# The gated MLP's up projection: the rest of each weight block from an accumulating fetch onto its negated head

## The chip, the cores and the metric

The kernel runs on one core of a Trainium2 chip. The metric is the device time of one launch in microseconds (us), as the median of several runs; the runs shown here were 954.19, 954.41 and 954.55 us. Beside them stands one profiled execution, whose span from the first to the last instruction is 952.6 us. Engines are called as in the profile: PE is TensorE (PEld its weight loads), DVE is VectorE, ACT is ScalarE, POOL is GpSimd, and SP is SyncE, which issues most of the transfers.

## What is computed

One layer of a hybrid decoder on 512 tokens of 1024 channels: three token mixers, a gated merge, an output projection, and a gated MLP with a short causal convolution. The change touches the MLP's first product, `h2 @ w_up`, whose weights are 1024 x 6144 numbers of 4 bytes.

```python
    h2 = rms_norm(x, norm_ffn[l])
    up = causal_dwconv(h2 @ w_up[l], ffn_conv_w[l], ffn_conv_b[l])
    gate_h, val_h = jnp.split(up, 2, axis=-1)
    x = x + (jax.nn.gelu(gate_h, approximate=True) * val_h) @ w_down[l]
return rms_norm(x, final_norm)
```

## The kernel before

**Products in three parts.** Every large product runs in a 4-byte format (`float32r`) that keeps 12 bits of each number. To hold more, each operand is kept as two tiles: its 12-bit head and the exact rest, which again fits the format. `split` (L92) makes them: ACT writes the head (L94, a copy with rounding), and DVE subtracts the head from the source (L95). `mm3` (L97) then multiplies head by head, head by rest, and rest by head, in that order: for a tile of 128 output channels and 8 tiles of input channels it first issues the 16 products of the weights' head and then the 8 of the weights' rest (L101, 24 matmuls in all).

**Units and steps.** The kernel is a list of units, each a block of weights and what PE does with it, with steps of other work between them. `unit` (L130) and `step` (L134) put them on the list, `weave` (L137) mixes them, and `emit` (L169) walks it. Ahead of a unit, `emit` calls `fetch` for the blocks up to two units later (`AHEAD`). `fetch` (L149) issues the load of a block into a buffer `raw` on SP's queue (L152; there are three such buffers) and the `split`. Blocks with `parts` 1 have their head and rest in `whi` and `wlo`, of which there are three each. Blocks with `parts` 2 have them in four half-size tiles `r` out of a common pool of 53 slots of 128 x 512 numbers (L77), from which most activations come too. Buffers are handed out in the order of the program; the order of the instructions on each engine is fixed by a planner before the run, by that same order as far as a buffer and the operands are expected to be free.

**The MLP** runs in three groups (L958). Each group has 16 up units (`up_units`, L928), two for each of 8 tiles of hidden channels (one for the gate half, one for the value half), and then 8 down units (`down_units`, L855), which add the group's part of the second product to the residual `x2`. An up unit is 24 matmuls with `h2` as the activations, and `up_done` (L918): the convolution of three taps over the product (one ACT instruction, L910, two DVE instructions, L912), and for each second unit the gelu (L922, ACT), the product of both halves (L923, DVE) and a `split` of the result.

**The entry to the MLP.** The first three up units of the first group are `early` ones (L933, `parts` 2): they run the first 256 tokens while the norm of the last tokens is still being made. `norm2` and `norm2_flip` (L883, L887) make the normed activations: a mean square (ACT), some small steps (DVE), two scalings (DVE, L877), a transposition on PE (L895) and a `split` into `h2h` and `h2l`. The other 13 units of the first group and all 32 of the other two have `parts` 1: 45 units in all.

**The end.** Behind the last down units `final` (L949) makes the last norm and stores the result; it holds the one arithmetic instruction that POOL has in the MLP (L951).

Of the kernel before, what the change touches and what calls it, by code (L numbers as in the profile page):

```python
# [20 lines left out]
KD = D // P  # L21
# [17 lines left out]
AHEAD = 2  # L39
BRANCHES = (2, 0, 1)  # L40
# [3 lines left out]
# columns of the packed per-channel parameters  # L44
# [10 lines left out]
def trunk(ctx: ExitStack, tc: tile.TileContext, x, xT, mem, memT, par, wdecay, wch, wvd, wvg, wmk,  # L55
# [35 lines left out]
    # ---------------------------------------------------------------- helpers  # L91
    def split(hi, lo, src, eng=None):  # L92
        """src as its 12-bit head and the exact rest."""
        nc.scalar.activation(hi, src, AF.Copy)  # L94
        (eng or nc.vector).tensor_tensor(out=lo, in0=src, in1=hi.bitcast(F32), op=ALU.subtract)  # L95

    def mm3(ps, terms, first=True, last=True):  # L97
        """ps (+)= sum of lhsT.T @ rhs over (lhsT_hi, lhsT_lo, rhs_hi, rhs_lo)."""
        seq = [p for a, b, c, d in terms for p in ((a, c), (a, d))] + [(b, c) for a, b, c, d in terms]
        for i, (l, r) in enumerate(seq):  # L100
            nc.tensor.matmul(ps, lhsT=l, rhs=r, start=first and i == 0,  # L101
                             stop=last and i == len(seq) - 1)

    def rsqrt(v):
        """1 / sqrt(v) of [p, n] positive numbers: a guess from the exponent, three Newton steps."""
        n = v.shape[-1]
        y, h, t = stat(n), stat(n), stat(n)
        yi = y.bitcast(I32)
        nc.vector.tensor_scalar(out=yi, in0=v.bitcast(I32), scalar1=1, scalar2=None, op0=ALU.logical_shift_right)
        nc.vector.tensor_scalar(out=yi, in0=yi, scalar1=-1, scalar2=0x5F3759DF, op0=ALU.mult, op1=ALU.add)  # L110
        nc.vector.tensor_scalar(out=h, in0=v, scalar1=-0.5, scalar2=None, op0=ALU.mult)
        for _ in range(3):
            nc.vector.tensor_tensor(out=t, in0=y, in1=y, op=ALU.mult)
            nc.vector.tensor_tensor(out=t, in0=t, in1=h, op=ALU.mult)
            nc.vector.scalar_tensor_tensor(out=y, in0=t, scalar=1.5, in1=y, op0=ALU.add, op1=ALU.mult)
        return y

    def meansq(src, acc, width):
        """acc = sum of src^2 / width along the rows."""
        junk = small.tile([P, src.shape[-1]], BF16, tag="junk", name=nm("junk"), bufs=2)  # L120
        nc.scalar.activation(junk, src, AF.Square, scale=width ** -0.5, accum_out=acc)

    # ---------------------------------------------------------------- the program: a list of units, each a block
    # of weights and what the tensor engine does with it, and of steps of other work between them. A unit's
    # weights are fetched and split two units ahead of it.
    prog = []
    loads = []
    behind = {}  # loads issued behind the weights of a unit

    def unit(dram, n, fn, parts=1):  # L130
        """fn(W): W(j, m) is the [128, n/m] hi and lo part j of m of the [128, n] block."""
        prog.append((dram, n, fn, parts))

    def step(fn):  # L134
        prog.append((None, 0, fn, 0))

    def weave(units, steps, lead=0):  # L137
        """The units with the steps spread evenly behind them, from unit `lead` on."""
        done, m = 0, max(1, len(units) - lead)
        for i, u in enumerate(units):  # L140
            unit(*u)
            upto = len(steps) * max(0, i + 1 - lead) // m
            for s in steps[done:upto]:
                step(s)
            done = max(done, upto)
        for s in steps[done:]:
            step(s)

    def fetch(dram, n, parts):  # L149
# [10 lines left out]
        for j in range(2):  # L160
            ts.append((rslot((p, h)), rslot((p, h))))
            split(*ts[j], raw[:, j * h:(j + 1) * h])
# [6 lines left out]
    def emit():  # L169
        units = [i for i, p in enumerate(prog) if p[0] is not None]  # L170
        ws, at = {}, 0
        for i, (dram, n, fn, parts) in enumerate(prog):
            if dram is None:
                fn()
                continue
            u = units.index(i)
            while at < len(units) and at <= u + AHEAD:
                p = prog[units[at]]
                ws[units[at]] = fetch(p[0], p[1], p[3])
                for h in behind.get(at, ()):  # L180
                    h()
                at += 1
            fn(ws.pop(i))

    # ---------------------------------------------------------------- constants
# [7 lines left out]
    # keeps the tensor engine busy, and its clock up, until the first loads are in  # L193
# [10 lines left out]
    def add_square(acc, a):  # L204
        """acc + a^2 / 1024, for the rows' mean squares"""
# [6 lines left out]
    def mean_square(acc, n):  # L212
        """[128, n] mean squares, plus eps, of n*128 rows from the sums over 1024/128 tiles of their transpose."""
# [6 lines left out]
    def row_bcast(rstd, n):  # L220
        """[128, n*128] tile whose column t*128+i holds rstd[i, t] in every partition."""
# [14 lines left out]
    def token_units(dram, n, lhs, nt, evac):  # L236
        """Units for evac(t, psum[128 tokens, n]) of activations @ a block of n columns of weights, 256 rows each."""
# [11 lines left out]
    def token_held(dram, n, lhs, nt, evac, between=None):  # L249
        """The same, one tile of tokens after the other, with all weights held."""  # L250
# [15 lines left out]
    # ---------------------------------------------------------------- x: norm  # L266
    # the queries of the memory attention are made from x before its rows' 1/rms is known (it scales the scores);
    # everything else is made from the normed x in hh, hl
# [37 lines left out]
    def start():  # L306
        """The first two blocks of weights, beside the loads of x: the products run as it arrives."""
# [35 lines left out]
    # ---------------------------------------------------------------- memory: keys and values  # L343
    # the rows' 1/rms is applied to the products
# [3 lines left out]
    def mem_load(i):  # L348
        """Half i of the memory's transpose: head and rest with the norm's gain, sums of squares."""
# [38 lines left out]
    def keys(i, ps):  # L388
        f = fslot((P, MEM))
        nc.vector.tensor_tensor(out=f, in0=ps, in1=mst["rb"], op=ALU.mult)  # L390
        # a tile that two heads share is kept once for each, zero in the other's rows
# [8 lines left out]
    # per pair of heads: [h0 0:192 | 0 (64) | h1 0:192 | unused]  # L400
# [9 lines left out]
    def value_units(pr):  # L410
        # the split of these weights is shared with GpSimd
# [19 lines left out]
    # ---------------------------------------------------------------- input projection, channel-major  # L431
    # tiles of wch: 0-5 queries of the memory attention, 6-9 blocks 0-3 of the recurrence, 10-13 q heads,
    # 14-17 k heads (6-17 each with 32 more channels, of blocks 4-7), 18-41 gates
# [5 lines left out]
    # depthwise convolution of the recurrence  # L439
# [13 lines left out]
    def piece(ps, i):  # L453
        """The 32 channels of blocks 4-7 that sit beside 96 others in the product i of 12."""
# [17 lines left out]
    # ---------------------------------------------------------------- memory attention  # L472
# [48 lines left out]
    # ---------------------------------------------------------------- merge of one branch  # L521
# [3 lines left out]
    def branch(n, acts, d, gt=None):  # L525
        """Units that add branch n's gated projection to channels d of the merge."""
# [20 lines left out]
    # ---------------------------------------------------------------- RG-LRU  # L547
    lsc, nsc = const.tile([P, NB], F32, name="lsc"), const.tile([P, NB], F32, name="nsc")

    def lru_rate():  # L550
        # C * log_sigmoid(lambda), with log1p(e) = 2 atanh(e / (2 + e))
# [45 lines left out]
    def lru_square(b):  # L597
        # 1 - a^2 = tanh(-log a) (1 + a^2)
# [10 lines left out]
    # 128-row tiles of the recurrence's output: block i and piece i of the others, then the rest  # L609
# [37 lines left out]
    # ---------------------------------------------------------------- gated linear attention  # L647
# [8 lines left out]
    # causal mask of the [j, i] scores  # L656
# [9 lines left out]
    # values and output gates token-major, the low-rank decay input beside the first values  # L666
# [55 lines left out]
    def decay_apply(h):  # L722
        """Chunks of 128 tokens. Within one, decays are taken relative to its middle, so that no exponent spans
        more than 64 of them upwards."""
# [43 lines left out]
    def state(n, hp):  # L768
        """State of a pair of heads behind chunk n."""
# [68 lines left out]
    # ---------------------------------------------------------------- output projection, residual  # L838
# [16 lines left out]
    def down_units(wd, acts, after=None, between=None):  # L855
        """x2 += acts.T @ [1024, 1024] weights"""
# [48 lines left out]
    # ---------------------------------------------------------------- gated MLP  # L905
# [22 lines left out]
    def up_units(g, acts, early=0):  # L928
        us = []
        first = []  # L930
        for n in range(16):
            i, half = 8 * g + n // 2, n % 2
            if n < early:  # L933
                # the first tiles' first tokens are ready before the others
# [9 lines left out]
            else:  # L944
                us.append((wup[NF * half + i], D,
                           lambda w, i=i, half=half: up_done(channel_major(w, KD, h2k), i, half, acts)))
# [22 lines left out]
def _layouts(np, v):  # L969
# [3 lines left out]
    def rows(a):  # L973
        """[K, C] -> [128, K/128, C]"""
        return a.reshape(a.shape[0] // P, P, a.shape[1]).transpose(1, 0, 2)

    def chan(a):
        """[K, n*128] -> [n, 128, K/128 * 128]"""
# [3 lines left out]
    def tok(a, c):  # L982
        """[1024, n*c] -> [n, 4, 128, 2 * c]"""
# [3 lines left out]
    def cols(a):  # L987
        """[n*128] -> [128, n]"""
# [10 lines left out]
    def blocks(a):  # L999
        """[768] -> [96, 8]"""  # L1000
# [50 lines left out]
```

## Time and profile before

| | us |
|---|---|
| median of three runs | 954.41 |
| lowest and highest | 954.19, 954.55 |
| span of the profiled execution | 952.6 |
| PE busy in it | 940.8 |
| DVE busy | 572.4 |
| ACT busy | 452.8 |
| POOL busy | 11.1 |

The profiled execution has no time of its own beside its span; 954.41 - 952.6 = 1.8 us of a run lie outside the span. An engine's busy time is the union of its instructions; the issuing of transfers isn't counted as busy. In the answers of the trace, a row like "559.54 384.30 PE mm L101 x1728" of the chain of work is a start, a length in us, the engine, the tile and the line, and how many instructions were merged. A row of the groups gives the line, the engine, the operation, output and inputs, the shape, the count, then the busy time in us and the mean of one in ns, then the idle time ahead of them.

### The profile page before, as it was taken

The numbers are of one execution on the slowest core, as the hardware profiler recorded it, in microseconds if no ns is written. First come the engines' busy times: TensorE is split into PE (matmuls) and PEld (weight loads), VectorE is DVE, ScalarE is ACT, GpSimd is POOL, SyncE is SP. The second block draws the span as 40 slices with busy tenths as digits, with TensorE's granted clock in tenths as the row PEclk, the third lists the DMA queues.
The fourth block names the chain that finished last, engine by engine and source line by source line (L and its number), as shares of the span: only waits on it lengthen the run. The fifth ranks groups of instructions, "written<-read, shape, count | busy, mean of one in ns | idle before, by whom it ended". The sixth has DMA issues, their size and how long they took to land.

```text
span 952.6 us, 11687 instructions
## 1 busy us (share of the span) xinstructions
PE 940.8 (99%) x4522; PEld 798.2 (84%) x4522; DVE 572.4 (60%) x1003; ACT 452.8 (48%) x682; POOL 11.1 (1%) x27
## 2 busy tenths in 40 slices
PE   8999999999999999999999999999999999999996
PEld 6899888887897789998888898888888888888885
DVE  7897754565744774485576756663456643556646
ACT  7565645684955783343334434442244432344432
POOL 0000000000000000000000000000000000000002
PEclk9999999999999999999999999999999999999998
DMA  7446212222232232222266202232232332322312
GB/s 231 152 138 193 67 57 68 80 92 78 75 117 79 77 99 84 78 94 72 67 197 224 77 23 88 89 105 95 90 109 89 97 102 90 107 93 91 131 45 88
DMA packets 30839, 95.95 MB, mean 101 GB/s; under 512 B 3568, under 2 KB 4736, under 8 KB 30784
## 3 DMA queue, kind: packets, MB, share of 16 engines
q1 hardware_dynamic: 30208, 94.16, 30.7%
q10 hardware_dynamic: 576, 1.05, 0.3%
q8 instruction: 35, 0.57, 0.2%
q14 instruction: 20, 0.16, 0.1%
HBM read 93.10 MB, written 2.10 MB: 100 GB/s over the span
## 4 chain that ended last, share of the span: by engine, by line
PE 95%; DVE 3%; DMA 0%; ACT 0%; issue 0%; SPq 0%; DVEq 0%; ACTq 0%
PE mm L101 89%; PE sm L101 3%; PE mm L328 1%; DVE wlo L95 1%; PE sm L787 1%; DMA m<-in_xT 0%; DVE r L95 0%; PE sm L789 0%; PE sm L773 0%; DVE m L296 0%; PE sm L760 0%; PE sm L895 0%; PE sm L808 0%; DVE hl L95 0%; PE sm L502 0%
## 5 line engine op out<-in xcount | busy, mean ns | idle before, releaser
L95 DVE TENSOR_TENSOR wlo<-raw,whi 128x1024 fp32r<-128x1024 f32 (+3 forms) x171 | 189.2, 1110 | 215.7 <-PE mm L101 98.6
L94 ACT ACTIVATE whi<-raw 128x1024 fp32r<-128x1024 f32 (+3 forms) x171 | 164.6, 966 | 198.1 <-PE mm L101 176.4
L101 PE MATMUL mm<-h2l,whi 128*128 128x512 f32 x360 | 140.1, 389 | 0.0
L101 PE MATMUL mm<-h2h,whi 128*128 128x512 f32 x360 | 139.9, 389 | 0.0
L101 PE MATMUL mm<-whi,r 128*128 128x512 f32 (+1 forms) x448 | 135.3, 381 | 0.0
L101 PE MATMUL mm<-hh,whi 128*128 128x512 f32 x288 | 113.9, 396 | 0.0
L101 PE MATMUL mm<-hl,whi 128*128 128x512 f32 x288 | 112.6, 391 | 0.0
L101 PE MATMUL mm<-r,whi 128*128 128x512 f32 (+1 forms) x448 | 98.3, 368 | 0.0
L101 PEld LDWEIGHTS mm<-whi,r 128*128 128x128 f32 x448 | 83.7, 188 | 15.0
L101 PEld LDWEIGHTS mm<-r,whi 128*128 128x128 f32 x448 | 77.9, 189 | 14.6 <-issue 0.8
L101 PE MATMUL mm<-h2h,wlo 128*128 128x512 f32 x360 | 88.9, 389 | 0.0
L101 PE MATMUL mm<-wlo,r 128*128 128x512 f32 (+1 forms) x224 | 85.6, 382 | 0.2 <-DVE wlo L95 0.2
L101 PEld LDWEIGHTS mm<-h2l,whi 128*128 128x128 f32 x360 | 67.6, 188 | 14.0
L101 PEld LDWEIGHTS mm<-h2h,wlo 128*128 128x128 f32 x360 | 67.6, 188 | 14.0
L101 PEld LDWEIGHTS mm<-h2h,whi 128*128 128x128 f32 x360 | 67.5, 188 | 13.9
L912 DVE SCALAR_TENSOR_TENSOR f<-mm,prm,f 128x511 f32<-128x511 f32 x96 | 71.7, 746 | 7.8 <-ACT f L910 6.1
L101 PE MATMUL mm<-hh,wlo 128*128 128x512 f32 x288 | 71.2, 389 | 0.0
L101 PEld LDWEIGHTS mm<-hh,whi 128*128 128x128 f32 x288 | 54.1, 188 | 11.6 <-issue 0.4
L101 PEld LDWEIGHTS mm<-hh,wlo 128*128 128x128 f32 x288 | 54.1, 188 | 11.2
L101 PEld LDWEIGHTS mm<-hl,whi 128*128 128x128 f32 x288 | 54.1, 188 | 10.7
L94 ACT ACTIVATE r<-f 128x512 fp32r<-128x512 f32 (+4 forms) x47 | 27.2, 589 | 65.0 <-DVE f L923 61.8
L101 PE MATMUL mm<-r,r 128*128 128x512 f32 (+1 forms) x240 | 56.8, 391 | 0.0
(191 smaller groups left out, 1208.0 us busy)
## 6 DMA issues: line engine op xcount, KB each, us to landing
raw<-in_wup SPq DMA_DIRECT2D x48, 512.0 KB, 3.5
raw<-in_wch SPq DMA_DIRECT2D x40, 512.0 KB, 3.3
raw<-in_wdown SPq DMA_DIRECT2D x24, 512.0 KB, 3.5
raw<-in_wbr SPq DMA_DIRECT2D x24, 384.0 KB, 3.1
raw<-in_wvg SPq DMA_DIRECT2D x12, 384.0 KB, 3.0
raw<-in_wout SPq DMA_DIRECT2D x8, 512.0 KB, 3.5
raw<-in_wmk SPq DMA_DIRECT2D x6, 512.0 KB, 3.4
raw<-in_wmv SPq DMA_DIRECT2D x8, 384.0 KB, 3.1
```

Source lines behind the costliest of these rows:

```text
L94: nc.scalar.activation(hi, src, AF.Copy)
L95: (eng or nc.vector).tensor_tensor(out=lo, in0=src, in1=hi.bitcast(F32), op=ALU.subtract)
L101: nc.tensor.matmul(ps, lhsT=l, rhs=r, start=first and i == 0, stop=last and i == len(seq) - 1)
L328: nc.tensor.matmul(ps[u], lhsT=a, rhs=b, start=q == 0 and i in (0, 2), stop=q == KD - 2 and i >= len(seq) - 2)
L787: nc.tensor.matmul(ps[:, j, :], lhsT=sT[h][:, t, :], rhs=vt[t][hp][:, j, :], start=True, stop=t == 0)
L912: nc.vector.scalar_tensor_tensor(out=a[:, j:], in0=ps[:, :S - j], scalar=col(C_FCW + 48 * (2 - j) + f), in1=a[:, j:], op0=ALU.mult, op1=AL ...
```

## The change

The 45 up units that had `parts` 1 get `parts` 4. For these `fetch` makes the rest in another way: ACT writes the head `hi` and, by a second instruction for each half, the negated head into the tile of the rest `lo`; POOL then issues a second transfer of the same half of the block from memory (256 KB) that adds what it reads to what lies in `lo`. The DVE subtraction of these blocks is gone. Head and rest of these blocks are four half-size tiles of the pool of 53 slots, no longer `whi` and `wlo`. The blocks are fetched four units ahead (`FAR`) instead of two. `emit` is rewritten so that units may differ in this: each unit carries what is due ahead of it and how far; what is due at one unit is issued in the order of the units that it is for. All other units keep `AHEAD`. A helper `made_unit`, which nothing calls, is added as well, and comments are dropped.

```diff
@@ -37,11 +37,12 @@
 NSLOT = 53
 NWB = 3
 AHEAD = 2
+FAR = 4
...
     def unit(dram, n, fn, parts=1):
...
-        prog.append((dram, n, fn, parts))
+
+        w = {}
+        i = sum(1 for k, *_ in prog if k == "unit")
+
+        def ready():
+            w["w"] = fetch(dram, n, parts)
+            for h in behind.get(i, ()):
+                h()
+        prog.append(("unit", [(FAR if parts == 4 else AHEAD, ready)], lambda: fn(w["w"])))
...
     def step(fn):
-        prog.append((None, 0, fn, 0))
+        prog.append(("step", [], fn))
...
@@ -159,7 +171,14 @@
         ts = []
         for j in range(2):
             ts.append((rslot((p, h)), rslot((p, h))))
-            split(*ts[j], raw[:, j * h:(j + 1) * h])
+            if parts == 4:
+
+                hi, lo = ts[j]
+                nc.scalar.activation(hi, raw[:, j * h:(j + 1) * h], AF.Copy)
+                nc.scalar.activation(lo, raw[:, j * h:(j + 1) * h], AF.Copy, scale=-1.0)
+                nc.gpsimd.dma_start(lo, dram[:, j * h:(j + 1) * h], accum_op=ALU.add)
+            else:
+                split(*ts[j], raw[:, j * h:(j + 1) * h])
...
     def emit():
-        units = [i for i, p in enumerate(prog) if p[0] is not None]
-        ws, at = {}, 0
-        for i, (dram, n, fn, parts) in enumerate(prog):
-            if dram is None:
-                fn()
-                continue
-            u = units.index(i)
-            while at < len(units) and at <= u + AHEAD:
-                p = prog[units[at]]
-                ws[units[at]] = fetch(p[0], p[1], p[3])
-                for h in behind.get(at, ()):
-                    h()
-                at += 1
-            fn(ws.pop(i))
...
+        units = [p for p in prog if p[0] == "unit"]
+        due = {}
+        for v, (_, pre, _) in enumerate(units):
+            for lead, fn in pre:
+                due.setdefault(max(0, v - lead), []).append((v, fn))
+        u = 0
+        for kind, _, fn in prog:
+            if kind == "unit":
+                for _, f in sorted(due.pop(u, ()), key=lambda d: d[0]):
+                    f()
+                u += 1
+            fn()
...
@@ -943,7 +960,7 @@
                 us.append((wup[NF * half + i], D, fn, 2))
             else:
                 us.append((wup[NF * half + i], D,
-                           lambda w, i=i, half=half: up_done(channel_major(w, KD, h2k), i, half, acts)))
+                           lambda w, i=i, half=half: up_done(channel_major(w, KD, h2k), i, half, acts), 4))
```

More of the change, by code (lines that the diff above doesn't have):

```diff
@@ L130, in unit, with made_unit @@
     def unit(dram, n, fn, parts=1):
-        prog.append((dram, n, fn, parts))
+        w = {}
[5 more added lines that the diff above has]
+        prog.append(("unit", [(FAR if parts == 4 else AHEAD, ready)], lambda: fn(w["w"])))
+    def made_unit(pre, fn):
+        prog.append(("unit", pre, fn))
     def step(fn):
-        prog.append((None, 0, fn, 0))
+        prog.append(("step", [], fn))
     def weave(units, steps, lead=0):
```

## The prediction

> **What bounds the kernel now.** I read the page's first lines, then the chain of work in order of time, then the groups of the stretch that the change touches.
>
> ```profile
> span 952.6 us, 11687 instructions
> PE 940.8 (99%) x4522; PEld 798.2 (84%) x4522; DVE 572.4 (60%) x1003; ACT 452.8 (48%) x682; POOL 11.1 (1%) x27
> PEclk9999999999999999999999999999999999999998
> ```
>
> PE is busy for 940.8 of 952.6 us at its full clock. DVE, which the change relieves, is idle for 40% of the span. The question is whether PE ever waits for DVE where the work goes away. The chain from the last units before the MLP to the end:
>
> ```profile
> 470.95 66.67 PE mm L101 x294
> ...
> 552.67 5.75 PE mm L101 x48
> 558.42 0.45 PE sm L895 x4
> 558.87 0.02 issue
> 558.89 0.60 ACT h2h L94
> 559.50 0.04 issue
> 559.54 384.30 PE mm L101 x1728
> 943.87 0.70 DVE m L858
> ```
>
> From 559.54 to 943.84 us the chain is one piece of 1728 matmuls: all up and down units, with no wait for another engine. The only wait at the entry is for an ACT head of the activations, 0.60 us at 558.89. The wait table of PE has one row that bears on the MLP:
>
> ```profile
> PE mm L101 <- ACT h2h L94: 0.3, 1, 0.3
> ```
>
> Could the matmuls themselves go faster with less traffic on DVE? Of the 1728, 72 are the second token halves of the three early units; they start 0.12 us apart:
>
> ```profile
> 566.22 0.28 PE L101 MATMUL mm<-h2l,r 128*128 128x256 f32 x1
> 566.34 0.28 PE L101 MATMUL mm<-h2h,r 128*128 128x256 f32 x1
> ```
>
> That is 8.64 us. The other 1656 (45 up units and 24 down units of 24) have 512 columns: (384.30 - 8.64) / 1656 = 0.2268 us each. The piece of 294 matmuls at 470.95, all of 512 columns, gives 66.67 / 294 = 0.2268 us. Most of it lies in these two stretches, where transfers were heavy; the third row is the start of the MLP (columns: stretch, its length, busy time and count of PE, PEld, DVE, ACT and POOL, clock, share of the DMA engines, GB/s):
>
> ```profile
> 476.00:500.00 24.00, 24.00 (x107) 19.89 (x106) 16.89 (x24) 8.91 (x12) 0.00 (x0) 1.00 0.61 195
> 500.00:537.60 37.60, 37.60 (x168) 31.07 (x168) 24.79 (x45) 16.31 (x29) 0.00 (x0) 1.00 0.58 190
> 559.50:655.00 95.50, 95.45 (x455) 80.53 (x456) 53.46 (x65) 39.17 (x49) 0.00 (x0) 1.00 0.26 85
> ```
>
> The matmul takes the same 0.2268 us with the DMA engines at 0.6 and DVE at 70% as with them at 0.26 and DVE at 56%. So one unit takes 24 x 0.2268 = 5.44 us whatever stands beside it, and the MLP is at PE's own pace already.
>
> **The change part by part.** The groups of the stretch from 559.5 to 943.9 us:
>
> ```profile
> L95 DVE TENSOR_TENSOR wlo<-raw,whi 128x1024 fp32r<-128x1024 f32 x62 | 76.0, 1225 | 127.2 <-PE mm L101 79.9 <-ACT whi L94 47.2
> L94 ACT ACTIVATE whi<-raw 128x1024 fp32r<-128x1024 f32 x62 | 65.4, 1055 | 75.4 <-PE mm L101 75.4
> L910 ACT ACTIVATE f<-mm,prm 128x512 f32<-128x512 f32 x48 | 37.4, 780 | 28.7 <-PE mm L101 28.7
> L912 DVE SCALAR_TENSOR_TENSOR f<-mm,prm,f 128x510 f32<-128x510 f32 x48 | 35.9, 748 | 1.7
> L923 DVE TENSOR_TENSOR f<-f,f 128x512 f32<-128x512 f32 x24 | 16.6, 692 | 0.8
> L922 ACT ACTIVATE f<-f 128x512 f32<-128x512 f32 x24 | 15.2, 632 | 45.8 <-DVE f L912 45.8
> L94 ACT ACTIVATE r<-f 128x512 fp32r<-128x512 f32 x24 | 15.2, 632 | 61.8 <-DVE f L923 61.8
> L94 ACT ACTIVATE r<-raw 128x512 fp32r<-128x512 f32 x8 | 4.6, 621 | 3.7 <-DMA raw<-in_wdown 3.7
> ```
>
> *Removed:* 45 DVE subtractions of 1.225 us, 55.1 us; DVE goes from 572.4 to about 517 us. None of it is in the chain, and no stall goes with it: worth 0.
>
> *Moved to ACT:* for each of the 45 blocks one head of 1.055 us becomes four instructions of 128 x 512 at 0.621 us, 2.48 us: +1.43 us a unit, +64 us in all; ACT goes from 452.8 to about 517 us. Within an up unit ACT then has 2.48 + 0.78 + (0.632 + 0.632) / 2 = 3.9 us of 5.44. It has 1.5 us to spare in every unit, and what it does late only holds a product's bank, of which there are five. Cost 0 in the steady part. The cover is those 1.5 us; were ACT to need over 5.44 us, each of 45 units would pay the excess.
>
> *Added:* 90 accumulating transfers of 256 KB from POOL's queue. Nothing is queued on POOL behind them but the multiplication L951 at the end, for which all up units are long done. SP's queue keeps its 48 loads. A `raw` buffer now comes free after ACT's fourth instruction and not after DVE, which costs SP nothing.
>
> What the trace does not show is an accumulating transfer, or any transfer from POOL. Call d the spacing at which they finish one behind the other. The nearest rows:
>
> ```profile
> raw<-in_wup SPq DMA_DIRECT2D x48, 512.0 KB, 3.5
> m<-in_x SPq DMA_DIRECT2D x8, 256.0 KB, 3.0
> L152 SPq DMA_DIRECT2D raw<-in_wup x48: 327/328/328, 512.4 to 869.0; - x48
> ```
>
> From below, d is the 0.33 us that SP takes to issue a load; from above, twice the 3.0 us of a plain 256 KB load from issue to landing, for a transfer that reads two sources and overlaps nothing: 6.0 us. What d must stay under: a unit needs two, and its rests are wanted only for the last 8 of its matmuls. With a lead of four units (21.8 us), the 32 transfers of a full group have 16 x 5.44 + 21.8 = 108.8 us: d may be 3.4 us. In the first group 26 have 13 x 5.44 + 21.8 = 92.5 us, 3.6 us each. I take d below 3.0 us, because plain loads do overlap: at 195 GB/s (the row at 476) a load of 512 KB (524 thousand bytes) lands every 2.7 us, though each takes 3.5. Then the transfers lie under the matmuls: 0. The engines' time, too:
>
> ```profile
> q1 hardware_dynamic: 9628, 34.53, 27.2%
> ```
>
> This row is of the MLP's stretch alone (packets, MB, share). 0.272 x 384.4 = 104.6 us for 34.53 MB, so 1.6 us of all engines for a 512 KB load and 0.8 us for 256 KB. A unit with both costs 1.6 + 2 x 0.8 = 3.2 us of 5.44, and 4.8 us if an accumulating one costs double.
>
> On that point the Trainium skill, "DMA: Bandwidth & Descriptors", section "Two DMAs through the same engine are not ordered", reports that a read-modify-write packet directly behind another of the same row mostly read stale data, so such packets overlap in an engine. No run here shows it; by it d is near the plain load's and the sum is the same.
>
> A rule that speaks against the change: the Trainium skill, "SBUF — State Buffer", section "SBUF: two separate sides", says that GpSimd can't write a transfer's descriptors while DVE runs an instruction in a two-port mode, such as a copy. The rows above show no copy among DVE's work in an up unit, so by the rule as stated the sum stays; if it held for all DVE work there (2 x 0.75 and half of 0.69 + 0.69 us), POOL would have 3.2 of each 5.44 us and an issue longer than about 2 us would set the pace.
>
> *Moved, the entry.* Units 0 to 2 are early ones with tiles from the common pool; units 3 to 5 had `whi` and `wlo`, written well ahead of the norm. Now their tiles come from the pool too, in program order. Unit 3 (issued ahead of the last output-projection unit) still gets its slots early: 16 merged tiles, 16 held weights, three blocks of 4 and up to 8 normed tiles make 52 of 53. Units 4 and 5 come behind the normed tiles of the last tokens, as unit 2 does now, and these are written at 553.70:
>
> ```profile
> 552.27 1.09 ACT L94 ACTIVATE h2h<-sm 128x512 fp32r<-128x512 f32 x2 [0.93 <-PE sm L895]
> 553.25 1.15 ACT L94 ACTIVATE r<-raw 128x512 fp32r<-128x512 f32 x2
> 558.89 1.09 ACT L94 ACTIVATE h2h<-sm 128x512 fp32r<-128x512 f32 x2 [4.50 <-PE sm L895]
> ...
> 553.70 1.42 DVE L877 SCALAR_TENSOR_TENSOR f<-m,st,gain 128x512 f32<-128x512 f32 x2
> ```
>
> ACT's 4.5 idle us before 558.89 take what is new: behind unit 2's heads (to 554.4) four instructions for unit 4 (to 556.8) and four for unit 5 (to 559.2). The head `h2h` for which PE waits is ready to go at 558.87 and would start at 559.2: **+0.3 us**. Bounds: 0, if the planner puts it ahead; +2.7 us, if unit 6's four (2.4 us) stand ahead of it as well.
>
> **Sum:** 952.6 + 0.3 = 952.9 us of span; with the 1.8 us outside it (954.41 - 952.6) **954.7 us**.
>
> **The rivals.**
>
> *Accumulation sets the pace (slower).* Should d exceed 3.4 us, the rests come late, PE waits at the rest's first matmul of nearly every up unit, and the matmul chain breaks. The excess is 26d - 92.5 in the first group and 32d - 108.8 in each of the others, 90d - 310 in all: 50 us at d = 4 (1004.7 us in all), 230 us at d = 6 (1184.7). For it: no row shows such a transfer, it fetches the block again, reads its destination too and is issued by an engine that has issued none. Against it: even if the DMA engines set d, and some 20 plain loads take 32 of the 108.8 us, (108.8 - 32) / 32 = 2.4 us of engine time are left for each, three times that of a plain 256 KB.
>
> *ACT blocks the entry (slower).* Unit 6's instructions ahead of `h2h`: 954.4 + 2.7 = 957.1 us. Against it: its `raw` buffer is unit 2's, free only when DVE has made unit 2's rests at about 557.5, and the load then takes 3.5 us.
>
> *DVE's relief shows (faster).* All that is to be had is the 0.67 us from 558.87 to 559.54 and what PE idles behind it, 0.05 us in the row at 559.50: 953.7 us, within 0.2%. More needs matmuls closer than 0.2268 us, which no row has. If DVE's rest isn't what PE waits for, the relief is simply hidden, and that is the forecast.
>
> **How the numbers follow.** A measurement can tell about 0.2%, 1.9 us, from no change. Forecast (953 to 956.3 us) 0.65; ACT at the entry by over 1.9 us 0.10; accumulation 0.21; faster by over 1.9 us 0.04. So faster 0.04, same 0.65, slower 0.31. The first two cases hold 0.75; the range takes in the near end of the third, up to d = 3.6 us (90 x 3.6 - 310 = 14, so 969 us): 953 to 969.
>
> **What would show it.** In the changed kernel's chain one piece of about 1728 matmuls of about 384 us, begun some 0.3 us later; DVE near 517 us, ACT near 517 us, DMA share in the up units 0.5 or more; no row of PE waiting for a transfer into `r`. If the chain breaks at matmuls of the rest with a transfer named as releaser, the second case holds, and its spacing gives d. If `h2h` waits for ACT by 2 us or more, the third does. A matmul spacing other than 0.2268 us would make the whole argument wrong.

## The result, and the profile after

The changed kernel takes 961.22 us (960.98 to 961.80), the kernel before 954.45 us beside it: a ratio of 1.0072, with a 95% interval of 1.0058 to 1.0087. It is 6.8 us slower. The profiled execution has a span of 959.7 us, 7.1 us more than before. From its page, the first lines, the granted clock, and the queue of the accumulating transfers:

```profile
span 959.7 us, 11979 instructions
...
PE 944.3 (98%) x4522; PEld 802.5 (84%) x4522; DVE 521.2 (54%) x958; ACT 497.5 (52%) x817; POOL 90.1 (9%) x117
...
PEclk9999999999999999999999989999999999999999
...
q0 software_dynamic: 12960, 23.60, 14.6%
```

DVE has lost 51 us of work, and the kernel is slower all the same. One digit of the clock's row is an 8, a little behind the middle, which was a 9 before. The chain of work says where the time is:

```profile
556.15 0.61 DVE r L96
556.78 4.68 DMA raw<-in_wup
561.48 0.63 ACT r L177
562.11 0.52 ACT r L178
562.63 0.52 ACT r L177
563.15 0.52 ACT r L178
563.67 0.49 ACT h2h L95
564.20 386.74 PE mm L102 x1728
```

(L177 and L178 are the head and the negated head of an accumulated block, L95 and L102 the old L94 and L101.) The piece of 1728 matmuls is still one piece: no rest of a weight came late. But it begins at 564.20 instead of 559.54 us, 4.66 us later, and takes 386.74 instead of 384.30 us, 2.44 us longer. The sum, 7.10 us, is the whole loss of the span.

The first part is read from ACT's own timeline at that place:

```profile
557.53 0.62 ACT L177 ACTIVATE r<-raw 128x512 fp32r<-128x512 f32 x1
558.05 0.62 ACT L178 ACTIVATE r<-raw 128x512 fp32r<-128x512 f32 x1
561.48 0.63 ACT L177 ACTIVATE r<-raw 128x512 fp32r<-128x512 f32 x1 [2.81 <-DMA raw<-in_wup]
...
563.58 1.06 ACT L95 ACTIVATE h2h<-sm 128x512 fp32r<-128x512 f32 x2
```

The wait table of PE has this wait (total, times, longest):

```profile
PE mm L102 <- ACT h2h L95: 4.8, 1, 4.8
```

ACT is done with units 4 and 5 at about 558.7 us. Then it sits idle for 2.81 us with the next block's load as the releaser, does that block's four instructions, and only then makes `h2h`, for which PE waits. The block is unit 6's, and the head stands behind it in ACT's fixed order. The second part shows in the windows (columns as in the prediction: the stretch, its length, busy time and count of PE, PEld, DVE, ACT and POOL, PE's clock, the share of the DMA engines, GB/s):

```profile
559.00:564.20 5.20, 0.41 (x4) 0.17 (x2) 0.02 (x1) 2.72 (x6) 1.92 (x3) 0.87 0.99 306
564.20:567.60 3.40, 3.40 (x14) 3.20 (x15) 1.27 (x2) 0.44 (x1) 0.62 (x1) 0.50 1.11 252
567.60:571.00 3.40, 3.40 (x22) 3.40 (x22) 0.00 (x0) 0.48 (x1) 0.00 (x0) 0.69 1.10 268
571.00:576.00 5.00, 5.00 (x43) 5.00 (x42) 1.93 (x3) 2.88 (x4) 0.00 (x0) 1.00 0.10 18
```

PE is idle for nearly five microseconds, and when it starts again its clock is at half, 0.50; some five and a half microseconds later it is back at 1.00. In the same stretch the DMA engines are taken completely, so the slow matmuls could also be laid to the transfers; the experiments separate the two.

### The profile page after: what moved, and what is told of

It is laid out like the page before. It is cut to its first block, busy times and chain, and to the rows that moved or that the text cites. A ratio compares the mean times of both kernels' runs of the same rounds, so it can differ in the third digit from the quotient of the medians.

```text
span 959.7 us, 11979 instructions
## 1 busy us (share of the span) xinstructions
PE 944.3 (98%) x4522; PEld 802.5 (84%) x4522; DVE 521.2 (54%) x958; ACT 497.5 (52%) x817; POOL 90.1 (9%) x117
## 4 chain that ended last, share of the span: by engine, by line
PE 94%; DVE 3%; DMA 1%; ACT 1%; issue 0%; SPq 0%; ACTq 0%
PE mm L102 87%; PE sm L102 3%; PE mm L345 1%; DVE wlo L96 1%; DVE r L96 1%; PE sm L804 1%; DMA raw<-in_wup 0%; PE sm L806 0%; PE sm L790 0%; DVE m L313 0%; DMA raw<-in_wch 0%; PE sm L777 0%; PE sm L825 0%; DVE hl L96 0%; PE sm L519 0%
## 5 line engine op out<-in xcount | busy, mean ns | idle before, releaser
L102 PE MATMUL mm<-h2h,r 128*128 128x512 f32 (+1 forms) x816 | 242.3, 380 | 4.8 <-ACT h2h L95 4.8
L96 DVE TENSOR_TENSOR wlo<-raw,whi 128x1024 fp32r<-128x1024 f32 (+3 forms) x126 | 134.1, 1069 | 137.3 <-ACT whi L95 95.9
L95 ACT ACTIVATE whi<-raw 128x1024 fp32r<-128x1024 f32 (+3 forms) x126 | 117.2, 935 | 159.7 <-PE mm L102 127.7
L102 PEld LDWEIGHTS mm<-h2h,r 128*128 128x128 f32 x816 | 152.0, 191 | 33.1 <-ACT h2h L95 5.0
L102 PE MATMUL mm<-h2l,r 128*128 128x512 f32 (+1 forms) x408 | 153.2, 379 | 0.0
L102 PE MATMUL mm<-whi,r 128*128 128x512 f32 (+1 forms) x448 | 135.3, 381 | 0.0
L179 POOL DMA_DIRECT2D r<-in_wup x90 | 77.9, 870 | 462.5 <-ACT r L178 437.6
L102 PE MATMUL mm<-hh,whi 128*128 128x512 f32 x288 | 113.9, 396 | 0.0
L102 PE MATMUL mm<-hl,whi 128*128 128x512 f32 x288 | 112.6, 391 | 0.0
L102 PE MATMUL mm<-r,whi 128*128 128x512 f32 (+1 forms) x448 | 98.3, 368 | 0.0
L102 PEld LDWEIGHTS mm<-whi,r 128*128 128x128 f32 x448 | 83.7, 188 | 15.0
L102 PEld LDWEIGHTS mm<-r,whi 128*128 128x128 f32 x448 | 77.9, 189 | 14.5 <-issue 0.8
L102 PEld LDWEIGHTS mm<-h2l,r 128*128 128x128 f32 x408 | 77.9, 191 | 14.1
L102 PE MATMUL mm<-wlo,r 128*128 128x512 f32 (+1 forms) x224 | 85.6, 382 | 0.2 <-DVE wlo L96 0.2
L102 PE MATMUL mm<-hh,wlo 128*128 128x512 f32 x288 | 71.2, 389 | 0.0
L177 ACT ACTIVATE r<-raw 128x512 fp32r<-128x512 f32 x90 | 55.7, 619 | 19.1 <-DMA raw<-in_wup 19.1
L927 ACT ACTIVATE f<-mm,prm 128x512 f32<-128x512 f32 x48 | 37.0, 770 | 54.5 <-PE mm L102 54.5
L102 PEld LDWEIGHTS mm<-hh,whi 128*128 128x128 f32 x288 | 54.1, 188 | 11.6 <-issue 0.4
L102 PEld LDWEIGHTS mm<-hh,wlo 128*128 128x128 f32 x288 | 54.1, 188 | 11.2
L102 PEld LDWEIGHTS mm<-hl,whi 128*128 128x128 f32 x288 | 54.2, 188 | 10.7
L95 ACT ACTIVATE r<-f 128x512 fp32r<-128x512 f32 (+4 forms) x47 | 27.2, 589 | 58.0 <-DVE f L940 55.1
```

Of the source, the lines that this page charges most:

```text
L177: nc.scalar.activation(hi, raw[:, j * h:(j + 1) * h], AF.Copy)
L179: nc.gpsimd.dma_start(lo, dram[:, j * h:(j + 1) * h], accum_op=ALU.add)
L927: nc.scalar.activation(a, ps, AF.Identity, scale=col(C_FCW + 96 + f), bias=col(C_FCB + f))
```

## The experiments

The first theory: the loss is ACT held up at the entry, and the clock that falls in the wait; the accumulating fetches themselves cost nothing. The main rival: accumulation, or POOL's queue, costs time somewhere in the steady part.

**Unit 6 behind the head.** One block's fetch is moved in program order; all accumulation stays.

```diff
-    def unit(dram, n, fn, parts=1):
+    def unit(dram, n, fn, parts=1, lead=None):
...
-        prog.append(("unit", [(FAR if parts == 4 else AHEAD, ready)], lambda: fn(w["w"])))
+        prog.append(("unit", [(lead or (FAR if parts == 4 else AHEAD), ready)], lambda: fn(w["w"])))
...
-                           lambda w, i=i, half=half: up_done(channel_major(w, KD, h2k), i, half, acts), 4))
+                           lambda w, i=i, half=half: up_done(channel_major(w, KD, h2k), i, half, acts), 4,
+                           3 if g == 0 and n == 6 else None))
```

> The changed kernel, but unit 6 of the first group is fetched three units ahead instead of four, so that its four ACT instructions stand behind the head h2h of the last tokens on ACT; everything else, the accumulating fetches of all 45 blocks included, stays. Theory (the whole loss is ACT held up at the entry by unit 6's late load, and PE's clock falling in that wait): h2h starts at about 558.9 us, PE waits some 0.7 us, the matmul piece behind it takes 384.3 us again: 954.5 us, 6.7 us less than the changed kernel. Rival (the accumulating fetches cost time in the steady part, or POOL's use costs at the ends): 957 us or more.

Measured: 954.33 us against 954.59 before, ratio 0.9998 (0.9989 to 1.0007). Its chain:

```profile
558.74 0.60 ACT h2h L95
...
559.39 384.30 PE mm L102 x1728
```

Two of its windows, one right behind the entry and one over the last units of the first group and up units of the second:

```profile
561.00:564.40 3.40, 3.40 (x31) 3.40 (x30) 0.32 (x1) 0.78 (x1) 0.00 (x0) 1.00 1.03 291
...
664.00:751.00 87.00, 87.00 (x385) 72.03 (x385) 28.50 (x38) 48.22 (x85) 25.58 (x30) 1.00 0.79 187
```

The matmuls take 384.30 us, the number of the kernel before to the last digit, with 90 accumulating transfers under them and the DMA engines at 0.79. At the entry they are at 1.03 and 291 GB/s while the clock stays 1.00. So the whole loss was the place of four ACT instructions, and the rival falls. The kernel isn't faster than before either: DVE's relief is worth nothing.

**A lead of two.**

```diff
-FAR = 4
+FAR = 2
```

> The changed kernel with a lead of two units for the accumulated blocks (FAR = 2). ACT's order then has units 4 and 5 ahead of h2h, but not unit 6. Theory: no long wait at the entry, 954.5 us, if the rests still land in time: ACT 2.5 us, two issues of 1.04 us and 7.2 us to landing make about 12 us, and two units with 16 matmuls of the next give 14.5 us. Rival (the accumulating fetch needs the longer lead): PE waits at the rests of the up units; 1 us in each of 45 would make 1000 us.

Measured: 967.37 us (964.07 to 970.01), ratio 1.0132 (1.0112 to 1.0152). At the entry the theory held: `h2h` starts at 559.16 us, and PE waits 0.2 us for it. The forecast of 954.5 us was wrong all the same. PE's row of the wait table, of the profiled execution (the shortest of the four, with a span of 962.4 us), and the chain at one of its four places:

```profile
PE mm L102 <- DMA r<-in_wup: 6.7, 4, 2.4
```

```profile
764.01 6.18 DMA r<-in_wup
770.24 82.81 PE mm L102 x364
```

With the shorter lead the rests do come late, though not in every unit: a few times, by up to 2.4 us. ACT's timeline shows why at this place:

```profile
758.05 1.06 ACT L95 ACTIVATE whi<-raw 128x1024 fp32r<-128x1024 f32 x1 [3.93 <-DMA raw<-in_wdown]
761.00 0.63 ACT L95 ACTIVATE r<-f 128x512 fp32r<-128x512 f32 x1 [1.89 <-DVE f L940]
761.54 0.61 ACT L177 ACTIVATE r<-raw 128x512 fp32r<-128x512 f32 x1
762.06 0.61 ACT L178 ACTIVATE r<-raw 128x512 fp32r<-128x512 f32 x1
```

(L940 is the old L923, the product of both halves.) The negated heads stand behind a down block's load (3.93 us) and behind the split of an earlier product (1.89 us), and POOL's transfer then takes 6.18 us more. The other three waits come near the end of the up units of the first and the third group, behind the same two things (4.93 and 3.89 us for a down block's load, 1.89 us for the split). It is again the order on ACT that makes a head wait for a load that isn't its own.

The four waits are 6.7 of the 10.0 us by which this span exceeds the first experiment's 952.4. About 1.7 us more are the clock, which fell behind one of them. The first five matmuls behind the two longest waits:

```profile
636.22 2.12 PE L102 MATMUL mm<-h2h,r 128*128 128x512 f32 x5 [2.41 <-DMA r<-in_wup]
...
903.45 1.43 PE L102 MATMUL mm<-h2h,r 128*128 128x512 f32 x5 [2.36 <-DMA r<-in_wup]
```

Behind the wait of 2.41 us the clock is at 0.50 until about 640 us, and ten matmuls take 3.98 instead of 2.27 us; behind that of 2.36 us it stays at 1.00. The rest of the 10.0 us was not followed up. The three runs that weren't profiled took longer, and their granted clock is lower (0.995, 0.993 and 0.990, against 0.996), which would fit more such falls, but isn't shown.

**Matmuls in the gap.** The changed kernel, with work for PE while it waits.

```diff
+NFILL = 20
...
+                    xn3 = h2.get(("xn", 3))
                     if n != 1:
                         norm2_flip(2 + n // 2)
+                    if n == early - 1:
+                        fps = sbank((P, P))
+                        for _ in range(NFILL):
+                            nc.tensor.matmul(fps, lhsT=ident, rhs=xn3[1][:, 3 * P:], start=True, stop=True)
```

> The changed kernel with 20 matmuls of 128 x 128 (of the normed tokens, their product unused) behind the transpositions of the last tokens, where PE waits 4.8 us. Theory (the second part of the loss is PE's clock, which falls to half in the wait and stays so for some 6 us): the wait stays, but the clock stays at 1.0 and the 1728 matmuls take 384.3 instead of 386.7 us: 958.8 us. Rival (the slower matmuls come from the transfers of that stretch, whose share of the DMA engines is 1.1, and not from the idle time): 961.2 us, or more by what the fillers overrun.

Measured: 959.41 us, ratio 1.0050 (1.0036 to 1.0064). The chain's last pieces at the entry and two windows (the kernel has one line more, so L96, L97 and L103 are L95, L96 and L102 of the changed kernel):

```profile
563.55 0.49 ACT h2h L96
564.06 0.70 DVE h2l L97
564.81 384.18 PE mm L103 x1727
```

```profile
558.50:564.20 5.70, 5.12 (x46) 4.93 (x44) 0.14 (x1) 2.84 (x6) 2.07 (x3) 1.00 1.03 309
564.20:567.60 3.40, 3.06 (x24) 2.86 (x25) 1.15 (x2) 0.32 (x1) 0.51 (x1) 1.00 1.10 246
```

`h2h` is as late as in the changed kernel, but the clock stays at 1.00 beside the same transfers (1.03 and 1.10 of the engines), and the matmuls take 384.18 us. So it is the idle time that lowers the clock, and not the transfers. Of the 2.4 us some 0.6 are lost again at the entry, where the chain now goes on through DVE's rest `h2l` and the long piece begins at 564.81 instead of 564.20 us.

**Four raw buffers.**

```diff
-NRAW = 3
+NRAW = 4
```

> The changed kernel with four raw buffers instead of three. ACT's order is the same: unit 6's four instructions still stand ahead of h2h, but their load no longer waits for unit 2's buffer. Theory (three terms: ACT work of unit 6, the wait for its load, the clock): only the ACT work is left, 12 instructions of 0.52 us from 554.4 to 560.7 us, h2h 1.8 us late, no fall of the clock in a wait of some 2 us: 956.3 us. Rival (the load is late for another reason, the DMA engines being taken by the accumulating fetches): as the changed kernel, 961 us.

Measured: 957.54 us (955.87 to 958.41), ratio 1.0030 (1.0017 to 1.0042). Chain and windows:

```profile
560.26 0.52 ACT r L178
560.77 0.49 ACT h2h L95
561.31 385.80 PE mm L102 x1728
```

```profile
559.80:561.30 1.50, 0.00 (x0) 0.00 (x0) 0.01 (x1) 1.50 (x4) 1.14 (x3) 1.00 1.01 273
...
562.00:563.00 1.00, 1.00 (x7) 0.95 (x6) 0.57 (x1) 0.00 (x0) 0.00 (x0) 0.75 1.06 293
563.00:564.00 1.00, 1.00 (x7) 1.00 (x6) 0.00 (x0) 0.00 (x0) 0.00 (x0) 0.50 1.09 297
...
565.00:566.00 1.00, 1.00 (x6) 1.00 (x6) 0.00 (x0) 0.00 (x0) 0.00 (x0) 0.54 1.12 303
566.00:567.00 1.00, 1.00 (x11) 1.00 (x10) 0.00 (x0) 0.32 (x1) 0.00 (x0) 1.00 1.08 291
```

And PE's wait:

```profile
PE mm L102 <- ACT h2h L95: 1.9, 1, 1.9
```

The wait for the load is gone: ACT's instructions follow one another at 0.52 us, and `h2h` starts at 560.77 us, as the theory had it. But the clock falls here too, behind a wait of 1.9 us, and costs 385.80 - 384.30 = 1.5 us, which the theory had left out. So of the first part, 4.66 us, about 2.9 us (563.67 - 560.77) were the wait for the load, and the rest was ACT's work on the block (560.77 - 558.89 = 1.9 us).

**The same lead and tiles without accumulation.** DVE makes the rests again.

```diff
-                nc.scalar.activation(lo, raw[:, j * h:(j + 1) * h], AF.Copy, scale=-1.0)
-                nc.gpsimd.dma_start(lo, dram[:, j * h:(j + 1) * h], accum_op=ALU.add)
+                nc.vector.tensor_tensor(out=lo, in0=raw[:, j * h:(j + 1) * h], in1=hi.bitcast(F32), op=ALU.subtract)
```

> The changed kernel with the same lead of four units and the same pool tiles for the 45 blocks, but the rest made by two DVE subtractions of 128 x 512, and no accumulating fetch. ACT has two instructions a block instead of four, and its order then has the heads of units 4 and 5 ahead of h2h, and unit 6's behind it. Theory (what costs is the place of unit 6's instructions on ACT; lead and pool tiles alone cost nothing): 954.5 us. Rival (the lead of four, or the pool's slots, delay the entry): 957 us or more.

Measured: 954.40 us, ratio 0.9999 (0.9989 to 1.0008). Its chain:

```profile
559.41 0.61 ACT h2h L95
...
560.06 384.30 PE mm L102 x1728
```

Unit 6's two heads stand behind `h2h` here, from 560.75 us on. The lead of four and the pool's slots alone cost nothing. DVE is at 574 us again, and the time is that of the first experiment, where it was at 521 us.

**The kernel before with a late head.** 16 copies on ACT ahead of `h2h`, whose results nothing reads; no accumulating transfer.

```diff
                     first.append((w, channel_major(w, KD, h2k, 0, S // 2)))
+                    if n == early - 1:
+                        for _ in range(16):
+                            nc.scalar.activation(small.tile([P, HB], BF16, tag="junk", name=nm("junk"), bufs=2),
+                                                 h2["xn", 3][1], AF.Copy)
                     if n != 1:
```

> The kernel before, with 16 ACT copies of a normed tile into a scratch tile, which nothing reads, ahead of h2h of the last tokens; no accumulating fetch, nothing on POOL. ACT is held from about 555.1 us for 15 x 0.52 us and two more instructions, to some 563 us. Theory (a late h2h and the clock that falls in the wait are the whole loss): h2h some 4.5 us late, the matmul piece behind it 386.7 instead of 384.3 us: 961 us. Rival (the fall of the clock needs the heavy transfers of the changed kernel): 959 us with a matmul piece of 384.3 us.

Measured: 961.58 us, ratio 1.0076 (1.0059 to 1.0092). Chain and a window:

```profile
555.92 7.28 ACT junk L939 x14
563.20 0.49 ACT h2h L94
...
563.73 386.68 PE mm L101 x1728
```

```profile
563.00:567.00 4.00, 3.27 (x15) 3.26 (x16) 1.29 (x2) 1.16 (x3) 0.00 (x0) 0.50 0.00 0
```

A late head alone gives the loss of the change, with no transfer running beside the slow matmuls (share 0.00; in the 4.5 us before, in which PE waits, it is 0.19): the clock at 0.50, the piece of 386.68 us, and the time within 0.4 us of 961.22.

**The down blocks too.** The first experiment's kernel, with 20 of the 24 down blocks accumulated. The line that is new against that kernel:

```diff
-        weave(down_units(wdown[g], acts, final if g == 2 else None), [])
+        weave([(*u, 4) if len(u) == 3 else u for u in down_units(wdown[g], acts, final if g == 2 else None)], [])
```

> The kernel of the first experiment (unit 6 later), with 20 of the 24 down blocks made by accumulating fetches as well, at the same lead of four: 65 blocks instead of 45. Theory (an accumulating fetch takes 1.56 us of the DMA engines, 0.146 x 959.7 us / 90; with its load a unit takes 1.6 + 2 x 1.56 = 4.7 us of 5.44, and 2 x 1.04 us of POOL): the transfers still lie under the matmuls, 954.5 us. Rival (at 87% of the DMA engines in a row of units with no pause the rests land late): PE waits at rests, 957 us or more.

Measured: 954.37 us, ratio 1.0001 (0.9991 to 1.0010). A window over up and down units of the second group, and the queue:

```profile
745.00:790.00 45.00, 45.00 (x200) 37.28 (x199) 13.56 (x19) 28.69 (x53) 17.34 (x21) 1.00 0.90 215
```

```profile
q0 software_dynamic: 18720, 34.09, 20.6%
```

130 accumulating transfers take 0.206 x 952.9 / 130 = 1.51 us each of all engines. With the engines at 0.90 in a stretch of 45 us PE is busy throughout. DVE is down to 497.5 us and the time is still that of before.

## Why the prediction was right and where it was wrong

The time lies in the stated range, 953 to 969 us, but by luck. The likeliest case, no change (953 to 956.3 us), did not come. The range goes on to 969 us only for accumulating transfers that set the pace, and they didn't; the case that came, ACT at the entry, was priced at 957.1 us. The step that failed is the last of the working: "+0.3 us" at the entry, which measured 4.66 us, and behind it 2.44 us of slower matmuls, for which the sum has no term.

**DVE's work is off the path: right.** It went to 521 us (517 forecast), and where nothing else is in the way the time is that of before: 954.33, 954.40 and 954.37 us at 521, 574 and 497.5 us of DVE.

**A matmul takes 0.2268 us whatever runs beside it: right at the full clock,** and shown at DMA shares up to 0.90 over long stretches. What the prediction didn't consider is that a wait at the entry changes the clock behind it.

**ACT's load: right in kind, too large.** 517 us were forecast, 497.5 measured. The sum took four durations of 0.62 us for each block; instructions in a row start 0.52 us apart, since the end of one overlaps the next. For the same reason units 4 and 5 alone cost nothing: in the first experiment, where only they stand ahead of the head, ACT is done with them at 558.4 us, and `h2h` starts at 558.74, in time.

**The accumulating transfer: right.** The queue's row gives 0.146 x 959.7 / 90 = 1.56 us of all engines each, twice the 0.8 us of a plain 256 KB, and POOL issues them 1.04 us apart:

```profile
556.89 0.86 POOL L179 DMA_DIRECT2D r<-in_wup  x1 [0.18 <-issue]
557.93 0.86 POOL L179 DMA_DIRECT2D r<-in_wup  x1 [0.19 <-issue]
```

The tile's view has all 90 issues (least, median and longest in ns, the first and the last start):

```profile
L179 POOL DMA_DIRECT2D r<-in_wup x90: 853/862/1247, 522.5 to 889.2; - x90
```

That is far from 3.4 us, and no rest comes late in the changed kernel, so accumulation doesn't set the pace at the lead of four. (From issue to landing one takes 7.2 us in the median, more than the 6.0 us allowed for transfers that overlap nothing; but the two of a unit are issued 1.04 us apart, so they overlap.) The rival's price, though, was worked out as a pace alone. At the lead of two its formula would still allow (16 x 5.44 + 10.9) / 32 = 3.1 us, yet rests came late: what counted there was how late a single unit's chain of ACT, POOL and landing starts, at the end of each group. Of the rules weighed in the prediction, the Trainium skill, "SBUF — State Buffer", section "SBUF: two separate sides", was not put to the test, since no copy stands among DVE's work there. The wider form that the prediction priced, all of DVE's work, is not borne out: the median issue is 0.86 us and the longest 1.25 us.

**The entry: the mechanism was named, and then dismissed.** The rival that ACT blocks the entry had unit 6's four instructions ahead of `h2h`, which is what happened; it got a chance of 0.10. The argument against it was that unit 6's `raw` buffer comes free only at about 557.5 us and its load then takes 3.5 us. Those numbers were near (556.78 and 4.68 us), but they speak the other way. ACT's order is fixed before the run. A late load doesn't move its instructions back; it makes all that stands behind them wait. (Why the planner put unit 6 ahead of the head isn't shown; that it did is.) The rival's price was too small for the same reason: 2.7 us counted the instructions, which came to 1.9 us, and left out the wait for the load (2.9 us by the fourth experiment) and the fall of the clock (2.4 us). Together these are 7.2 us, against the 7.1 us by which the span grew. The load was slower than 3.5 us while the accumulating fetches of units 4 and 5 took the engines (a share of 0.99 in the window at 559). The median of all 48 such loads went from 3.5 to 5.4 us with the change, and is 3.5 us without accumulation in the fifth experiment, so the change seems to have lengthened the wait that it caused.

## What to carry to other kernels

Before an engine is relieved, look whether the chain ever waits for it: here three kernels with 497 to 574 us of DVE work have one time. Where a prefetch puts instructions on an engine, ask what stands behind them in its order when the load is late, above all at the entry of a stage where a short chain of norms and transpositions decides; moving a single block's fetch behind that head gave all of the 6.8 us back. With the lead of two the same thing came at the end of each group. And a fetch that passes through several engines needs its lead for the latest single chain, not for the average pace.

## What was not expected of the hardware

In the fourth experiment a wait of 1.9 us was enough to bring PE's clock to 0.50 for about three and a half microseconds, beginning about 1 us after PE had started again. The waits for the same head of 0.3 us in the kernel before and 0.2 us in the first experiment were not. But the length of a wait doesn't settle it: with the lead of two the clock fell behind the wait of 2.41 us, which had one of 0.39 us some 1.2 us ahead of it, and not behind those of 1.53 and 2.36 us. What else decides stays open. The Trainium skill, "TensorE: Matmul & The Clock Gate", section "HAM oscillation — how this bites in real kernels", gives the rule that gaps above some 3.4 us are to be avoided. The 4.8 us of the changed kernel fit it; the falls behind 1.9 and 2.41 us don't, and there the measurement decides. The runs of the fourth experiment go from 955.87 to 958.41 us, and the granted clock is 0.998 in the shortest and 0.996 in the others. That would fit a fall that doesn't come every time, but only one of them was profiled.
